# Letting the first up pass form its input factors three query blocks earlier, with two instead of three prepared weight blocks

## The chip, the cores and the metric

The kernel runs on one NeuronCore of a Trainium2 chip. The metric is device time in microseconds (us), the median over several runs of the whole program. Five engines work side by side, each on its own queue of instructions: TensorE (PE, matrix products; its weight loads are listed as PEld), VectorE (DVE), ScalarE (ACT), GpSimd (POOL) and SyncE (SP), which here issues all DMAs. PE writes its products to PSUM, in eight banks; all else lives in SBUF, where the kernel keeps 50 equal buffers that it calls units.

## What is computed

One layer of an encoder on 2048 positions of 1024 channels:

```
h = rms_norm(x) * (1 + sc_m) + sh_m
u, f, q, k, v = split(h @ w_in)
y = concat(s5_mixer(u), fourier_mixer(f), window_attention(q, k, v)) @ w_out
x = x + gt_m * rms_norm(y)
h = rms_norm(x) * (1 + sc_f) + sh_f
gate, val = split(dwconv3(h @ w_up))          # w_up: 1024 x 5632
x = x + gt_f * rms_norm((gelu(gate) * val) @ w_down)
```

The change concerns the place where attention ends and `h @ w_up` begins. Every product of float32 data is made of three float16 products (high by high, low by high, high by low), so each float32 tile is split once into a high and a low half: ACT makes the high half, DVE the low one.

## The kernel before

**Stages.** In the order of time: the input norm and the input projection, the S5 and Fourier mixers, attention, the output projection (`proj`), two up passes (`ffn`) and two down stages (`down`).

**Attention** (`att`) goes over 16 query blocks n of 128 positions; two workers take the even and the odd ones, with four PSUM banks between them. A block makes its scores on PE, adds the bias and takes the maximum on DVE (the `L1330` instructions), exponentials on ACT, splits on ACT and DVE, transposes on PE (evacuated by ACT and DVE in turn), the product with v on PE, and its evacuation by ACT (high) and DVE (low, the one `SCALAR_TENSOR_TENSOR` of shape 128x3x128). That evacuation sets the future `f_ya[n]`: "block n is out" below.

**Projection.** `proj` goes over four chunks c of 512 positions. Chunk c waits for `f_ya[4c]` to `f_ya[4c+3]`, then makes 192 products on PE. `post(c)` follows: it normalises, adds the residual, normalises again, mostly on DVE, and sets `f_hp[c]`.

**Up passes.** The products of `ffn` use seven instead of eight block products (a Strassen-Winograd form). Pass p takes chunks 2p and 2p+1. `hcomb(p)` forms the seven input factors of pass p: eight sums or differences and seven pairs of splits, in all 22 DVE instructions on 1024 columns each and 14 of ACT. `wcomb` forms the seven weight factors of one of 22 weight blocks i out of two 512 KB loads, with 8 DVE instructions, into four units (called W*i* below). Pass 0 forms them and also stores them; pass 1 loads them back (three loads of 512 KB and one of 256 KB). For each pass and block, PE makes 7 x 12 = 84 products of 128x512; `up_copy` (ACT) and three `up_add` (DVE) evacuate them; `up_act` does the convolution and the gate with five DVE instructions and stores the result. "Block i" below is an up block; query blocks are named as such.

**What sets the order.** A planner (`Sched`) runs all of these as generators against cost guesses, and emits instructions in the order of its clock, by priority; `yield ("w", f)` lets nothing behind it be emitted before f is set, `yield ("acq", sem, n)` takes n from a counting semaphore. The tile framework makes the queues of the engines from that. On the chip each engine then takes its queue in that order. The number of weight blocks in flight is the semaphore `lead`, with `W_LEAD` places, given back after the last product of a block. `hcomb(0)` starts when `post(0)` and `post(1)` are done and, as `H_GATE` is not 0, `f_ya[15]` is set.

The functions that the diff touches, with the line numbers of the profile:

Of the kernel before, what the change touches and what calls it, by code (L numbers as in the profile page):

```python
# [68 lines left out]
W_ON_V = 2  # L69
N_SL = 3  # L70
W_ADD, H_ADD, G_ADD, SSQ = "VVVV", "V", "VVVV", "V"
W_LEAD, W_RAW, U_PAIRS, D_LEAD, TAIL = 3, 1, 4, 6, 2
F_GATE, H_GATE, D_FROM = 0, 1, (1, 0, 2)
N_CH = 2
N_PE = (1,)
G_M2 = 8
# [126 lines left out]
class Builder:  # L203
# [1358 lines left out]
    def hcomb(self, p):  # L1562

        for i in range(2):
            yield ("w", self.f_hp[2 * p + i])
        (ya, ta), (yb, tb) = self.f_hp[2 * p].val, self.f_hp[2 * p + 1].val
        if p == 0 and H_GATE:
            yield ("w", self.f_ya[15])
        H = self.H[p] = {}
        if p:  # L1570
            self.f_ht = {r: [Fut(), Fut()] for r in (1, 5, 6, 2, 7, 3, 4)}
        t1_, t2_ = [self.u([2, 512]) for _ in range(2)], [self.u([2, 512]) for _ in range(2)]
        e = H_ADD

        def out(r, q, t, src):
            if q == 0:
                H[r] = [self.u([4, 512], F16) for _ in range(2)]
            sl = slice(2 * q, 2 * q + 2)
            t = yield from self.act(t, H[r][HI][:, sl], src, AF.Copy)
            t = yield from self.tt(t, H[r][LO][:, sl], src, H[r][HI][:, sl], ALU.subtract)  # L1580
            if q:
                self.f_H[p][r].set(t, H[r])
                if p:
                    for x in range(2):
                        t = yield from self.dma(t, self.h2d[r - 1, x].rearrange("p (a b) -> p a b", a=4), H[r][x])
                    self.f_h2[r].set(t)

        T = {}
        for q in range(2):
            T[1, q] = yield from self.tt(max(ta[q], tb[q]), t1_[q], yb[q], ya[q], ALU.subtract, eng=e)  # L1590
            yield from out(1, q, ta[q], ya[q])
        for q in range(2):
            tz = max(T[1, q], tb[q + 2])
            T[2, q] = yield from self.tt(tz, t2_[q], yb[q + 2], t1_[q], ALU.subtract, eng=e)
            yield from out(5, q, T[1, q], t1_[q])
        for q in range(2):
            T[3, q] = yield from self.tt(max(tb[q], tb[q + 2]), yb[q], yb[q + 2], yb[q], ALU.subtract, eng=e)
            yield from out(6, q, T[2, q], t2_[q])
        for q in range(2):
            yield from out(2, q, ta[q + 2], ya[q + 2])  # L1600
        for q in range(2):
            T[4, q] = yield from self.tt(max(ta[q + 2], T[2, q]), t2_[q], ya[q + 2], t2_[q], ALU.subtract, eng=e)
            yield from out(7, q, T[3, q], yb[q])
        for q in range(2):
            yield from out(3, q, tb[q + 2], yb[q + 2])
        for q in range(2):
            yield from out(4, q, T[4, q], t2_[q])
# [44 lines left out]
    def ffn(self):  # L1652
        A = self.A
        self.cwt, self.carry = self.const([P, 44, 4]), self.const([P, 44, 2])
        self.gx, self.wdd = self.const([P, 2, NFF]), self.dt([7, 11, P, 1024], F16)
        yield from self.dma(0, self.cwt, A["cw"])
        yield ("w", self.f_pc[F_GATE])
        wq, lead = [Fut() for _ in range(2 * NFF)], Sem(W_LEAD)
        self.sc.spawn(self.up_weights(wq, lead, Sem(W_RAW)))
        self.f_gr = [[Fut() for _ in range(NFF)] for _ in range(2)]  # L1660
        self.grd = self.dt([2, NFF, P, 1024], F32)
        self.f_up = [[Fut() for _ in range(NFF)] for _ in range(2)]
        self.f_wd = [Fut() for _ in range(11)]
        self.sc.spawn(self.down_weights(), 4)
        pairs = Sem(U_PAIRS)
        for p in range(2):
            fH = self.f_H[2 * p]
            gos = {}
            if p == 0:
                for r in (1, 5, 6, 2, 7, 3, 4):  # L1670
                    gos[r] = Fut()
                    self.sc.spawn(self.h_back(r, gos[r]), 0)
            for i in range(NFF):
                tp = yield ("acq", pairs, 1)
                tw = yield ("w", wq[NFF * p + i])
                W, ts = wq[NFF * p + i].val
                off = 1 + p
                U = [self.u([UB]) for _ in range(2)]
                n0, n1 = slice(off, off + 512), slice(off + 512, off + 1024)
                b1, b2, b3 = None, None, None  # L1680
                f = {r: Fut() for r in (1, 5, 6, 2, 7, 3, 4)}

                def prod(r, ps, t, first):
                    u, c = self.PLACE[r]
                    th = yield ("w", fH[r])
                    h = fH[r].val
                    t = max(t, th, ts[u])
                    for k in range(4):
                        sl = slice(k * P, k * P + P)
                        t = yield from self.mm3(t, ps, (W[u][:, HI, c, sl], W[u][:, LO, c, sl]),  # L1690
                                                (h[HI][:, k], h[LO][:, k]), first and k == 0, k == 3, r != 2)
                    if p == 0 and i == NFF - 1:
                        gos[r].set(t)
                    return t

                t = yield ("acq", self.bank["s"], 1)
                b1 = self.ps("s")
                t = yield from prod(1, b1, max(t, tp), True)
                self.sc.spawn(self.up_copy(t, b1, U[0][:, n0], f[1]))
                t = yield ("acq", self.bank["s"], 1)  # L1700
                b2 = self.ps("s")
                t = yield from prod(5, b2, t, True)
                self.sc.spawn(self.up_copy(t, b2, U[1][:, n1], f[5]))
                t = yield ("w", f[1])
                t = yield from prod(6, b1, t, False)
                self.sc.spawn(self.up_copy(t, b1, U[0][:, n1], f[6]))
                t = yield ("acq", self.bank["z"], 1)
                b3 = self.ps("z")
                t = yield from prod(2, b3, t, True)
                self.sc.spawn(self.up_add(t, b3, U[0][:, n0], f[1], f[2], True))  # L1710
                t = yield ("w", f[6])
                t = yield from prod(7, b1, t, False)
                self.sc.spawn(self.up_add(t, b1, U[1][:, n1], f[5], f[7], False))
                t = yield ("w", f[5])
                t = yield from prod(3, b2, t, False)
                self.sc.spawn(self.up_add(t, b2, U[0][:, n1], f[6], f[3], True))
                t = yield ("w", f[7])
                t = yield from prod(4, b1, t, False)
                self.sc.spawn(self.up_copy(t, b1, U[1][:, n0], f[4], True))
                lead.give(t)  # L1720
                self.f_up[p][i].set(t)
                self.sc.spawn(self.up_act(p, i, U, f, self.f_gr[p][i], pairs))
        yield from self.down()
# [386 lines left out]
```

## Time and profile before

| what | value |
|---|---|
| median of 3 runs | 2134.07 us (2133.83 to 2138.75) |
| the profiled execution | 2141.4 us, its span 2139.6 us |
| PE, DVE, ACT, POOL busy in the span | 1963.9, 1559.8, 991.0, 244.6 us |
| mean granted TensorE clock | 0.962 |
| query blocks 11, 12 and 15 out (DVE) | 767.3, 799.6, 840.3 us |
| both up passes end (PE) | 1701.8 us |

Times inside the span count from its first instruction. Busy time counts an engine while it executes. An idle stretch costs time only where it lies on the chain that ends last. In a row of the table by windows there stand, for one stretch, the busy time of each engine with the number of its instructions, the granted clock (1 is full speed) and the DMA share.

### The profile page before, as it was taken

What the parts mean: (1) busy time and instruction counts of PE and PEld (TensorE: products, weight loads), DVE (VectorE), ACT (ScalarE), POOL (GpSimd) and SP (SyncE); (2) the same over time, 40 slices, a digit from 0 to 9 for tenths busy, and PEclk for the clock granted to TensorE, in tenths of its full rate; (3) what the DMA queues carried; (4) which work ended last, traced back from release to release, by engine and by line L of the source; (5) the groups of instructions that cost most, each with busy time, mean ns of one, the idle gap of its engine ahead of it and who ended that gap; (6) DMA issues with size and microseconds to landing.
All of it is one profiled execution on the core that took longest, in us unless ns stands there. A gap on an engine that the chain in (4) does not pass through costs nothing.

```text
span 2139.6 us, 26850 instructions
## 1 busy us (share of the span) xinstructions
PE 1963.9 (92%) x9796; PEld 967.3 (45%) x9796; DVE 1559.8 (73%) x2305; ACT 991.0 (46%) x1666; POOL 244.6 (11%) x310
## 2 busy tenths in 40 slices
PE   6788888789988889997999999999999999999997
PEld 1336764444543444443444444444444444434445
DVE  8998898869677767899988875666565763547356
ACT  3643333355566576665555543444444433322221
POOL 1566554002000000000000000000000000011002
PEclk9989999899999989998999999999999999999998
DMA  9362145673746333346655566656565494548533
GB/s 368 105 209 61 56 127 162 217 247 137 256 144 220 126 125 133 136 179 249 223 197 187 188 216 260 230 189 226 201 217 201 158 334 157 162 134 300 177 100 113
DMA packets 206663, 397.27 MB, mean 186 GB/s; under 512 B 19521, under 2 KB 111938, under 8 KB 206530
## 3 DMA queue, kind: packets, MB, share of 16 engines
q1 hardware_dynamic: 206530, 395.55, 53.7%
q8 instruction: 77, 1.26, 0.2%
q14 instruction: 56, 0.46, 0.1%
HBM read 258.93 MB, written 134.98 MB: 184 GB/s over the span
## 4 chain that ended last, share of the span: by engine, by line
PE 49%; DVE 8%; ACT 2%; issue 1%; DMA 1%; POOL 0%; SPq 0%; POOLq 0%; DVEq 0%; ACTq 0%
PE ps L316 49%; DVE u L289 4%; DVE u L275 3%; ACT u L270 2%; DMA u<-d 0%; DMA u<-w_up 0%; DMA d<-u 0%; ACT L270 0%; POOL u L275 0%; SPq L265 0%; POOLq L2095 0%; DVE u L282 0%; ACT c L270 0%; DVEq L289 0%; DVEq L275 0%
## 5 line engine op out<-in xcount | busy, mean ns | idle before, releaser
L316 PE MATMUL ps<-u,u 128*128 128x512 f16 (+5 forms) x9030 | 1879.2, 368 | 90.7 <-DVE u L289 40.5
L316 PEld LDWEIGHTS <-u 128*128 128x128 f16 (+1 forms) x9058 | 846.8, 99 | 1035.4 <-issue 157.6
L275 DVE TENSOR_TENSOR u<-u,u 128x512 f32<-128x512 f32 (+10 forms) x584 | 506.6, 900 | 105.9 <-ACT u L270 92.4
L270 ACT ACTIVATE u<-u 128x1024 f16<-128x1024 f32 (+7 forms) x485 | 406.0, 869 | 360.9 <-DVE u L275 150.3
L270 ACT ACTIVATE u<-ps 128x512 f32<-128x512 f32 (+8 forms) x497 | 268.7, 555 | 410.4 <-PE ps L316 377.5
L289 DVE SCALAR_TENSOR_TENSOR u<-u,c,u 128x1023 f32<-128x1023 f32 (+5 forms) x248 | 291.3, 1197 | 61.2 <-ACT u L270 53.9
L289 DVE SCALAR_TENSOR_TENSOR u<-ps,u 128x512 f32<-128x512 f32 (+4 forms) x231 | 152.3, 666 | 229.2 <-PE ps L316 199.2
L289 DVE SCALAR_TENSOR_TENSOR u<-u,u 128x1024 f16<-128x1024 f32 (+6 forms) x225 | 240.6, 1093 | 61.4 <-ACT u L270 58.1
L275 POOL TENSOR_TENSOR u<-u,u 128x288 f32<-128x288 f32 (+9 forms) x169 | 187.4, 1123 | 609.3 <-DVE u L289 462.4
L270 ACT ACTIVATE u<-u,c 128x1023 f32<-128x1023 f32 (+3 forms) x106 | 123.5, 1166 | 142.5 <-DVE u L289 122.7
L305 POOL MEMSET u<- 128x1 f32 x88 | 8.6, 98 | 1118.0 <-DVE u L289 415.8
L270 ACT ACTIVATE u<-u,st 128x384 f32<-128x384 f32 (+3 forms) x192 | 107.5, 592 | 30.8 <-DVE st L282 17.3
L316 PEld LDWEIGHTS ps<-u,u 128*128 128x128 f32 (+1 forms) x532 | 91.1, 180 | 39.9 <-DVE u L275 16.8
L316 PE MATMUL ps<-u,c 128*128 128x512 f32 (+4 forms) x142 | 61.8, 551 | 43.5 <-DVE u L300 18.5
L316 PE MATMUL ps<-c,u 128*128 128x128 f16 (+1 forms) x568 | 59.6, 229 | 23.9 <-ACT u L270 18.5
L270 ACT ACTIVATE c<-u 128x2 f32<-128x2 f32 (+1 forms) x88 | 17.8, 202 | 132.3 <-DVE u L289 132.2
L275 DVE TENSOR_TENSOR u<-u 128x512 f32<-128x512 f32 (+8 forms) x136 | 67.8, 502 | 12.4 <-ACT u L270 11.6
L300 DVE TENSOR_TENSOR_SCAN u<-u,u 128x512 f32<-128x512 f32 (+1 forms) x60 | 68.6, 1152 | 0.5
L1330 DVE CUSTOM_DVE_ANT_0 u<-ps,u 128x384 f32<-128x384 f32 (+1 forms) x96 | 48.1, 536 | 23.8 <-PE ps L316 23.7
L289 DVE SCALAR_TENSOR_TENSOR u<-u,st,u 128x384 f16<-128x384 f32 (+1 forms) x96 | 54.6, 603 | 12.2 <-ACT u L270 12.0
L270 ACT ACTIVATE u<-u,c,c 128x512 f32<-128x512 f32 (+1 forms) x64 | 48.4, 804 | 22.3 <-DVE u L275 6.2
L316 PEld LDWEIGHTS ps<-u,c 128*128 128x128 f32 (+1 forms) x142 | 23.9, 190 | 72.6 <-issue 46.6
(52 smaller groups left out, 370.9 us busy)
## 6 DMA issues: line engine op xcount, KB each, us to landing
u<-d SPq DMA_DIRECT2D x226, 512.0 KB
d<-u SPq DMA_DIRECT2D x158, 512.0 KB
d<-u SPq DMA_DIRECT2D x111, 256.0 KB
u<-w_ada SPq DMA_DIRECT2D x48, 512.0 KB
u<-w_up SPq DMA_DIRECT2D x44, 512.0 KB
u<-d SPq DMA_DIRECT2D x66, 256.0 KB
u<-x SPq DMA_DIRECT2D x32, 512.0 KB
u<-d SPq DMA_DIRECT2D x24, 511.0 KB
```

The source lines that it names most:

```text
L270: self.S.activation(out, in_, func, **kw)
L275: (self.V if eng == "V" else self.G).tensor_tensor(out, a, b, op)
L289: self.V.scalar_tensor_tensor(out, a, s, b, op0, op1)
L300: self.V.tensor_tensor_scan(out, d0, d1, 0.0, ALU.mult, ALU.add)
L305: (self.V if eng == "V" else self.G).memset(out, v)
L316: self.PE.matmul(o, a, b, start=st, stop=sp, skip_group_check=chain)
L1330: V.tensor_tensor_reduce(out=s_, in0=o, in1=self.bias[h // 2][:, h % 2, bo:bo + nk * 128], op0=ALU.add, op1=ALU.max, scale=1.0, scalar=-3e ...
```

## The change

```diff
-W_LEAD, W_RAW, U_PAIRS, D_LEAD, TAIL = 3, 1, 4, 6, 2
-F_GATE, H_GATE, D_FROM = 0, 1, (1, 0, 2)
+W_LEAD, W_RAW, U_PAIRS, D_LEAD, TAIL = 2, 1, 4, 6, 2
+F_GATE, H_GATE, D_FROM = 0, 12, (1, 0, 2)
...
     def hcomb(self, p):
...
-        if p == 0 and H_GATE:
-            yield ("w", self.f_ya[15])
+        if p == 0:
+            yield ("w", self.f_ya[H_GATE])
...
     def ffn(self):
...
         pairs = Sem(U_PAIRS)
+        yield ("w", self.f_ya[15])
         for p in range(2):
```

`hcomb(0)` now waits for query block 12 instead of 15. The loop over up blocks gets a wait of its own for query block 15, which it had through the factors before. At most two weight blocks are in flight instead of three, in both passes. No instruction is added or removed; the planner puts them in another order.

On DVE's queue, from the evacuation of query block 12 on (the row of shape 128x3x128), stood the scores of query block 14 (L1330, 128x384) and evacuations of block 13's transposes:

```order
L289 SCALAR_TENSOR_TENSOR u_6411<-ps_6932,u_6410 128x3x128
L1330 ISA u_6982,st_6980<-ps_6981,u_3439 128x384
L1330 ISA st_6980 128x1
L1330 ISA u_6982,st_6980<-ps_6991,u_3439 128x384
L1330 ISA st_6980 128x1
L282 TENSOR_SCALAR u_6996<-ps_6997 128x512
L1330 ISA u_7008,st_6980<-ps_7007,u_3440 128x384
```

Behind the same evacuation stands now (u_4656, u_4657, u_5606 to u_5609 are the results of `post(0)` and `post(1)`):

```order
L289 SCALAR_TENSOR_TENSOR u_6388<-ps_6879,u_6387 128x3x128
L282 TENSOR_SCALAR u_6894<-ps_6914 128x512
L275 TENSOR_TENSOR u_6919<-u_5606,u_4656 128x1024
L275 TENSOR_TENSOR u_6639<-u_6639 128x512
L275 TENSOR_TENSOR u_6944<-u_4656,u_6943 128x1024
L275 TENSOR_TENSOR u_6920<-u_5607,u_4657 128x1024
L275 TENSOR_TENSOR u_6944<-u_4657,u_6943 128x1024
L275 TENSOR_TENSOR u_6921<-u_5608,u_6919 128x1024
L275 TENSOR_TENSOR u_6993<-u_6919,u_6992 128x1024
```

All 22 instructions of `hcomb(0)` stand there in one run, ahead of the scores of query block 14.

At the end of attention on the same queue, behind the last evacuation of query block 15, stood the first instructions of `hcomb(0)`:

```order
L282 TENSOR_SCALAR u_7364<-ps_7392 128x512
L289 SCALAR_TENSOR_TENSOR u_6411<-ps_7398,u_6410 128x3x128
L275 TENSOR_TENSOR u_7417<-u_5637,u_4656 128x1024
L275 TENSOR_TENSOR u_7437<-u_4656,u_7436 128x1024
L275 TENSOR_TENSOR u_7418<-u_5638,u_4657 128x1024
```

Now there stand the sums of squares of projection chunk 3 and `post(3)`:

```order
L282 TENSOR_SCALAR u_7453<-ps_7466 128x512
L289 SCALAR_TENSOR_TENSOR u_6388<-ps_7472,u_6387 128x3x128
L282 TENSOR_SCALAR u_7494<-u_7494 128x512
L275 TENSOR_TENSOR u_7494<-u_7494 128x512 x7
L289 SCALAR_TENSOR_TENSOR u_7765<-ps_7766,u_7765 128x512
L289 SCALAR_TENSOR_TENSOR u_7765<-u_7765 128x512
```

Between the last evacuations of query blocks 12 and 15 stand now, besides `hcomb(0)`, all 21 DVE instructions of `post(2)`, which stood behind query block 15 before. Weight block 2, which was formed ahead of query block 8, is formed after up block 0.

## The prediction

> **What bounds the kernel now.** I read the page's busy shares first, then the chain that ended last, then a table of windows cut at the marks around the change, and last the idle times on the timelines of PE and DVE.
>
> ```profile
> PE 1963.9 (92%) x9796; PEld 967.3 (45%) x9796; DVE 1559.8 (73%) x2305; ACT 991.0 (46%) x1666; POOL 244.6 (11%) x310
> 839.79 33.84 PE ps L316 x156
> 1067.76 634.07 PE ps L316 x2937
> ```
>
> PE is the bound over the whole span. The second and third line are pieces of the chain: from 839.79, when attention ends, the chain goes through PE, then for 200 us through DVE in small pieces, and from 1067.76 to 1701.83 through PE alone. A matmul there takes 634.07 / 2937 = 0.216 us and an up block of 84 takes 18.1 us. Whatever reaches 1067.76 later ends later by as much; nothing after it has slack. So the question is when the same work (9 up blocks done) is reached. The windows (us; then busy time of PE, PEld, DVE, ACT, POOL; granted clock; DMA):
>
> ```profile
> 739.55:767.27 27.72, 12.99 (x63) 7.04 (x63) 24.07 (x40) 17.94 (x35) 0.00 (x0) 0.57 0.33 113
> 767.27:799.53 32.26, 32.26 (x198) 16.99 (x197) 20.63 (x59) 28.39 (x63) 0.00 (x0) 1.00 0.43 131
> 799.53:815.93 16.40, 16.40 (x105) 8.92 (x104) 6.47 (x23) 6.23 (x18) 0.00 (x0) 1.00 0.22 73
> 815.93:833.22 17.29, 15.20 (x109) 8.58 (x106) 12.74 (x38) 14.65 (x38) 0.00 (x0) 1.00 0.67 235
> 833.22:840.25 7.03, 5.79 (x33) 2.95 (x34) 3.83 (x8) 3.69 (x8) 0.00 (x0) 0.76 0.49 168
> 840.25:900.77 60.52, 60.47 (x277) 27.33 (x276) 53.19 (x56) 37.73 (x51) 0.39 (x4) 1.00 0.35 122
> 900.77:927.30 26.53, 25.30 (x118) 11.33 (x116) 26.50 (x29) 15.17 (x22) 0.20 (x2) 1.00 0.39 149
> 927.30:949.10 21.80, 21.05 (x95) 9.20 (x94) 20.75 (x24) 16.78 (x24) 0.20 (x2) 1.00 0.55 193
> 949.10:979.22 30.12, 18.99 (x87) 8.29 (x86) 28.98 (x31) 17.35 (x24) 0.20 (x2) 0.86 0.51 204
> 979.22:1002.34 23.12, 21.28 (x87) 8.95 (x86) 21.12 (x24) 15.23 (x20) 0.39 (x4) 0.89 0.59 225
> ```
>
> The marks are DVE's: query blocks 10 to 15 out (first five rows), then the third `up_add` of up blocks 0 to 4. Two things are to be seen. From 799.5 to 840.3, the tail of attention, DVE works 23.0 of 40.7 us and waits the rest, while PE is nearly full, because projection chunk 2 fills it between attention's small products. From 840.3 to 900.8 PE is full (60.47 of 60.52), with projection chunk 3 and up block 0, and beside it DVE does `hcomb(0)` and `post(2)`. Then four up blocks take 101.6 us, of which DVE is busy 97.4, though PE needs only 4 x 18.1 = 72.4: there DVE is the bound.
>
> ```profile
> 752.22 0.29 PE L316 MATMUL ps<-c,u 128*128 128x128 f16 x1 [11.59 <-ACT u L270]
> 978.77 21.27 PE L316 MATMUL ps<-u,u 128*128 128x512 f16 x84 [10.70 <-DVE u L289]
> 1001.88 10.10 PE L316 MATMUL ps<-u,u 128*128 128x512 f16 x46 [1.84 <-DVE u L289]
> ```
>
> These are PE's longest waits there (idle time before the instruction, and what ended it, in brackets): two for DVE in the up blocks, and 11.59 us between query blocks 10 and 11, where `post(1)` sits in DVE's queue and no projection is left to fill PE. That place, the first window, is a model of what the change makes of the tail.
>
> **The change part by part.** First, what is moved into the tail. DVE takes its queue in order, so the run of `hcomb(0)` behind query block 12 is done before query block 14's scores. Because chunk 2 of the projection then ends before attention does, `post(2)` comes ahead of query block 15 too.
>
> ```profile
> 840.25 10.30 DVE L275 TENSOR_TENSOR u<-u,u 128x1024 f32<-128x1024 f32 x9
> 835.47 1.28 DVE L282 TENSOR_SCALAR u<-ps 128x512 f16<-128x512 f32 x2
> 869.49 0.43 DVE L282 TENSOR_SCALAR u<-u 128x512 f32<-128x512 f32 x1
> ```
>
> Nine 1024-column instructions take 10.30 us, 1.14 each; two of 512 columns take 1.28, 0.6 each in a row. Moved are 22 of `hcomb(0)` and 15 of `post(2)` at 1.14 = 42.2, and six smaller ones of `post(2)`, five at 0.6 and one at 0.4 = 3.4: 45.6 us. As a cross-check, the window 840.25 to 900.77 has 53.19 us in 56 instructions; 43 of these are the moved ones, and the other 13, of 512 columns at 0.6, are 7.8, which leaves 45.4.
>
> What of it lies beside waiting: the tail has 40.7 - 23.0 = 17.7 us of DVE gaps. If the moved work filled all of them, the tail would grow by 45.6 - 17.7 = 27.9; if none, by 45.6. The gaps come from the chain of each query block (PE, ACT and DVE in turn):
>
> ```profile
> 805.26 0.56 DVE L1330 CUSTOM_DVE_ANT_0 u<-ps,u 128x384 f32<-128x384 f32 x1 [5.65 <-PE ps L316]
> 814.96 0.17 DVE L275 TENSOR_TENSOR st<-st 128x6 f32<-128x6 f32 x1 [3.85 <-ACT u L270]
> 828.67 0.17 DVE L275 TENSOR_TENSOR st<-st 128x6 f32<-128x6 f32 x1 [3.04 <-ACT u L270]
> 839.78 0.56 DVE L289 SCALAR_TENSOR_TENSOR u<-ps,u 128x384 f16<-128x384 f32 x1 [3.02 <-ACT u L270]
> ```
>
> The first goes (PE will be long done), the last stays (nothing is left to put there), the two waits for exponentials stay in part, and ACT, with 14 splits of `hcomb(0)` and the affine steps of `post(2)` between, is slower to answer. In the model window DVE kept a gap of 27.72 - 24.07 = 3.7 us. I take about 6.5 for query blocks 13 to 15, less than three times the model's, as the run of `hcomb(0)` itself has no gap: 27.9 + 6.5 = +34.4, with ends of 27.9 and 45.6. Against it: in PE's new order 27 products of chunk 2 fewer stand ahead of query block 12's end (192 matmuls instead of 219 since query block 11's). At the 0.16 us per matmul of the window before 799.53 (32.26 / 198) that is -4.4. Query block 15 is out about 30 us later, near 870.
>
> Second, what is gained behind it. From query block 15 on PE needs chunk 3 and up block 0, 60 us whatever DVE does; DVE's queue has only 18 instructions there now (eight sums of squares of chunk 3, seven of `post(3)`, three `up_add`), some 12.5 us by the prices above, so its relief is hidden: 0. Between the third `up_add` of up blocks 0 and 4, DVE's queue holds 100 instructions instead of 102: weight blocks 2 to 5 instead of 3 to 6 (32 each), the same 32 of `up_act` and `up_add`, all 22 of `hcomb(1)` instead of 18, 14 of `post(3)` instead of 20. Four come at 1.14 and six go, four at 1.14, one at 0.6 and one at 0.4: -1, between -5 (better packing) and +5 (the two w_up loads stand behind stores of results on SP's queue, and a wait for one stops DVE). Behind up block 4 nothing of `hcomb(1)` is left on DVE; the last small waits of PE up to 1067.76 fall away, -2 (at most 2.4 by the timeline). PE's waits that cover the 200 us stay otherwise what they are.
>
> Third, weight block 2 no longer formed ahead of query block 8.
>
> ```profile
> 661.30:668.70 7.40, 6.55 (x31) 2.84 (x30) 6.78 (x8) 3.48 (x6) 0.00 (x0) 1.00 0.80 270
> ```
>
> That takes 6.8 us from DVE and 1 MB of loads from DMA, where PE is busy 6.55 of 7.40 us anyway: -0.5, between -6.8 and 0.
>
> Fourth, two blocks of weights in flight. In pass 0 a weight block is now finished within the up block just before its use, 5 to 10 us ahead. In pass 1 the reload takes the place of the previous block's:
>
> ```profile
> 1300.00:1400.00 100.00, 100.00 (x465) 45.38 (x464) 60.17 (x62) 42.64 (x67) 0.88 (x9) 1.00 0.60 209
> 1413.62 2.21 SPq L265 DMA_DIRECT2D u<-d  x4
> 1422.24 2.42 SPq L265 DMA_DIRECT2D u<-d  x4
> ```
>
> The four loads issued at 1413.62 feed pass 1's up block 8, which begins at 1701.83 - 14 x 18.1 = 1448, 34 us later; with one block less in flight they feed up block 7, 16 us later. 1.79 MB at even the mean 209 GB/s take 8.6 us, so the load hides; I take +0.5 for all 42 places, with 0 and +6 as ends.
>
> Last, the clock. PE is sparse in the longer tail, as in the model window, where the granted clock was 0.57. Behind the wait of 10.70 the window from 979.22 shows 0.89 over 23.12 us, 5 us at half rate, 2.5 lost. Chunk 3 begins right behind attention's own products, so I take +1.5. The Trainium skill ("TensorE: Matmul & The Clock Gate", Part 1: The HAM clock gate) says that an idle window of about 3.4 us drops the array to half rate; by it the gaps that this change opens would also slow attention's own matmuls, which is rival C below. The model window agrees on the rate, with 0.57.
>
> The sum: 34.4 - 4.4 - 1 - 2 - 0.5 + 0.5 + 1.5 = +28.5 us. On the profiled execution that makes 2141.4 + 28.5 = 2169.9; that one stands 7.3 above the median of 2134.07, so on the median it makes 2162.6. I say 2163.
>
> **The rivals.** A, faster: the first four up blocks are relieved. There PE waits some 18 us and runs some at half clock, worth about 20. If the tail filled all its gaps back to query block 11, it would be 43.7 (DVE busy in the four windows) + 45.6 - 4 (scores of query block 12 that now stand ahead of block 11's end) = 85.3 us against 73.0 elapsed, +12; together -8, 2126. For it speaks that PE waits for DVE there; against it that DVE's queue in these blocks shrinks by 1 us only. It decides if those 97 us fall under some 85: chance 0.05. B, a smaller loss: the tail packs as in A, the rest stays: +12, 2146. Against it stands that the waits for ACT belong to each query block: 0.12. C, the half clock lies on the chain: some 18 us of attention's PE work after query block 12 (37.4 in the three windows, less 88 products of chunk 2 at 0.216) doubles: +18, 2181. The model window, at 0.57, kept DVE's gap at 3.7 us, so most would hide: 0.08. D, two blocks starve an up pass: a load that lands more than 16 us after its issue stops PE; 1 us at each of 40 places is +40, 2203. PE at 100.00 with a lead of three says nothing on two: 0.07. The change does move what it says; the new order shows that.
>
> **How the numbers follow.** The likeliest, with 0.68, is the sum; its own ends are +16 (27.9 - 4.4 - 5 - 2.4) and +42 (45.6 - 4.4 and the clock), 2150 to 2176. The range takes in B below and half of C above: 2143 to 2180. A measurement tells about 0.3%, 6.4 us, from no change. Faster than that is A, 0.05; within it the weak end of B and some of A, 0.04; slower the rest, 0.91.
>
> **What would show it.** Right: query block 15 out near 870; PE idle some 30 us between 820 and 870; PE full for 60 us behind it; four up blocks that again take about 100 us; pass 1 without gaps. Wrong: query block 15 out before 855 (B), the four blocks in under 90 us (A), waits of PE for `DMA u<-d` or for DVE `wcomb` results behind up block 5 (D).

## The result, and the profile after

The changed kernel takes 2173.58 us (median of 4 runs, 2170.26 to 2174.66) against 2136.41 of the kernel before (4 runs, 2133.83 to 2140.11): ratio 1.017, 95% interval 1.0148 to 1.0192, 37 us slower. The forecast was 2163 in a range of 2143 to 2180; the sign and the size hold, but several of the terms behind them do not.

The first line is the page's busy shares (busy us, share, instructions); two long pieces of the chain follow (start, length, engine, line, count):

```profile
PE 1969.3 (91%) x9796; PEld 967.0 (45%) x9796; DVE 1560.9 (72%) x2305; ACT 997.2 (46%) x1670; POOL 241.9 (11%) x310
```

```profile
869.05 66.60 PE ps L316 x302
1065.16 666.59 PE ps L316 x3088
```

As before, the chain runs through PE from attention's end, then through small pieces of DVE, then through PE alone. Attention's end (839.79 before) comes 29 us later. ACT has four instructions more.

The windows, cut at the same marks (ends of the evacuation that puts a query block out, and of the third `up_add` of an up block): query blocks 10 to 15, up block 0, up block 4, up block 9, and a part of pass 1.

```profile
728.17:758.65 30.48, 18.03 (x91) 9.31 (x89) 27.35 (x54) 21.95 (x41) 0.00 (x0) 0.72 0.64 211
758.65:782.21 23.56, 23.22 (x147) 12.22 (x147) 16.21 (x43) 22.61 (x54) 0.00 (x0) 1.00 0.22 65
782.21:833.02 50.81, 34.86 (x174) 16.44 (x171) 41.23 (x59) 31.45 (x49) 0.00 (x0) 0.86 0.30 103
833.02:852.26 19.24, 12.35 (x64) 6.26 (x64) 16.57 (x30) 8.43 (x15) 0.00 (x0) 0.58 0.28 99
852.26:874.28 22.02, 9.43 (x47) 4.45 (x46) 12.15 (x25) 17.00 (x35) 0.20 (x2) 0.61 0.63 213
874.28:932.51 58.23, 58.23 (x270) 26.37 (x269) 13.42 (x19) 15.54 (x25) 0.20 (x2) 1.00 0.05 19
932.51:1030.42 97.91, 84.58 (x367) 36.52 (x366) 96.13 (x101) 63.71 (x86) 1.18 (x12) 0.96 0.60 226
1030.42:1120.44 90.02, 86.92 (x388) 38.58 (x387) 73.44 (x80) 48.28 (x70) 0.98 (x10) 0.96 0.53 195
1300.00:1400.00 100.00, 100.00 (x465) 45.40 (x464) 61.55 (x62) 43.59 (x68) 1.18 (x12) 1.00 0.71 261
```

Rows three to five are the tail, query block 12 to 15: 92.07 us instead of 40.72. PE works 56.64 of them and idles 35.4; before, it idled 3.3. DVE works 69.95 instead of 23.04, and its gaps have grown, from 17.7 to 22.1 us. The sixth row is the stretch behind attention, full on PE, with DVE busy for only 13.42 of 58.23 us, as forecast. The last shows pass 1 without a gap.

The same stretches of the kernel before, for the comparison below: query block 6 to 12, the tail, up block 0 to 4, up block 4 to 9.

```profile
642.36:799.61 157.25, 133.20 (x766) 68.34 (x766) 110.61 (x234) 107.56 (x217) 0.00 (x0) 0.90 0.48 158
799.61:840.33 40.72, 37.39 (x245) 20.47 (x244) 23.04 (x67) 24.66 (x61) 0.00 (x0) 0.96 0.46 157
900.86:1002.43 101.57, 86.62 (x380) 37.84 (x379) 97.34 (x103) 64.45 (x88) 0.98 (x10) 0.93 0.51 192
1002.43:1086.13 83.70, 81.29 (x376) 36.48 (x374) 77.00 (x84) 49.11 (x72) 0.98 (x10) 1.00 0.64 234
```

The account in us, from the marks of the two traces; from up block 9 on the distance stays at +34.3 to the end of pass 1. The forecast's +1.5 for the clock and +0.5 for pass 1 belong to no single row:

| stage | before | after | difference | forecast |
|---|---|---|---|---|
| up to query block 6 | 642.4 | 639.7 | -2.7 | 0 |
| query block 6 to 12 | 157.3 | 142.5 | -14.7 | -4.9 |
| query block 12 to 15 | 40.7 | 92.1 | +51.4 | +34.4 |
| query block 15 to up block 0 | 60.5 | 58.2 | -2.3 | 0 |
| up block 0 to 4 | 101.6 | 97.9 | -3.7 | -1 |
| up block 4 to 9 | 83.7 | 90.0 | +6.3 | -2 |

The first row is nothing of the change: over all traces here query block 6 is out between 639.1 and 644.3. So the comparisons below count from query block 6.

The longest waits of PE in the tail (idle time and what ended it in brackets):

```profile
814.89 1.44 PE L316 MATMUL ps<-u,u 128*128 128x384 f16 x4 [7.86 <-DVE st L1330]
827.53 3.64 PE L316 MATMUL ps<-u,u 128*64 128x384 f16 x14 [6.00 <-ACT u L270]
840.00 1.01 PE L316 MATMUL ps<-c,u 128*128 128x128 f16 x8 [3.69 <-DVE st L1330]
863.19 1.21 PE L316 MATMUL ps<-c,u 128*128 128x128 f16 x5 [10.79 <-ACT u L270]
```

The first is the run of `hcomb(0)`: the scores at 814.89 wait for banks that DVE empties only behind it. The last has `post(2)` ahead of it twice. Its pieces of the chain, in order:

```profile
852.26 1.28 ACT L270
853.56 0.60 ACT u L270
854.17 1.28 ACT L270
855.47 0.21 ACT st L270
855.68 6.91 ACT u L270 x18
862.63 4.62 ACT u L270 x9
867.30 1.08 PE ps L316 x7
```

The pieces of 1.28 us without a tile are loads of ACT's function table: each of `post(2)`'s two norms has one activation with a reciprocal root, it now stands between exponentials, and the table is changed to it and back. Behind query block 15's exponentials, from 859.05 on, eight affine steps of `post(2)` (5.9 us in three pieces) are mixed with the six splits for which PE waits. Among the groups by line of the tail (782.21 to 874.28) the loads have a row (count, busy us, mean ns, idle time before):

```profile
L270 ACT ACT_TABLE_LOAD x4 | 5.1, 1283 | 0.8 <-PE ps L316 0.7
```

They are the page's four added instructions of ACT, 5.1 us in all, each of them a piece of the chain: the program's text adds no instruction, but its new order does. The Trainium skill ("ScalarE activation tables: per-element evaluation and per-set limits", What a function is on this engine) says that two functions of different sets are one load of 1283 ns apart; the trace agrees, with a mean of 1283.

### The profile page after: what moved, and what is told of

Its sections match the earlier page's. It is cut to its first block, busy times and chain, and to the rows that moved or that the text cites. A ratio compares the mean times of both kernels' runs of the same rounds, so it can differ in the third digit from the quotient of the medians.

```text
span 2172.0 us, 26891 instructions
## 1 busy us (share of the span) xinstructions
PE 1969.3 (91%) x9796; PEld 967.0 (45%) x9796; DVE 1560.9 (72%) x2305; ACT 997.2 (46%) x1670; POOL 241.9 (11%) x310
## 4 chain that ended last, share of the span: by engine, by line
PE 54%; DVE 6%; ACT 2%; issue 1%; DMA 1%; POOL 0%; SPq 0%; POOLq 0%; DVEq 0%; ACTq 0%
PE ps L316 54%; DVE u L289 3%; DVE u L275 3%; ACT u L270 2%; DMA u<-d 0%; ACT L270 0%; DMA u<-w_up 0%; POOL u L275 0%; SPq L265 0%; DVE u L1330 0%; POOLq L2096 0%; ACT c L270 0%; ACT st L270 0%; DVE u L282 0%; DVEq L289 0%
## 5 line engine op out<-in xcount | busy, mean ns | idle before, releaser
L316 PE MATMUL ps<-u,u 128*128 128x512 f16 (+6 forms) x9030 | 1880.9, 369 | 100.2 <-DVE u L289 31.6
L316 PE MATMUL ps<-c,u 128*128 128x128 f16 (+1 forms) x568 | 61.8, 235 | 40.7 <-ACT u L270 31.8
L270 ACT ACTIVATE c<-u 128x2 f32<-128x2 f32 (+1 forms) x88 | 17.8, 203 | 135.7 <-DVE u L289 135.7
L1330 DVE CUSTOM_DVE_ANT_0 u<-ps,u 128x384 f32<-128x384 f32 (+1 forms) x96 | 48.0, 536 | 20.0 <-PE ps L316 18.0
```

What stands on the lines that cost most here:

```text
L270: self.S.activation(out, in_, func, **kw)
L316: self.PE.matmul(o, a, b, start=st, stop=sp, skip_group_check=chain)
L1330: V.tensor_tensor_reduce(out=s_, in0=o, in1=self.bias[h // 2][:, h % 2, bo:bo + nk * 128], op0=ALU.add, op1=ALU.max, scale=1.0, scalar=-3e ...
```

## The experiments

The theory after the result: the tail grows by the DVE work moved into it, with no gap to hide in; something else makes query block 12 early; and the lead of two costs a little in the up blocks. The change has three parts that can be separated: the lead, the wait of the loop over up blocks, and the place of `hcomb(0)`.

**The lead alone.** In the kernel before:

```diff
-W_LEAD, W_RAW, U_PAIRS, D_LEAD, TAIL = 3, 1, 4, 6, 2
+W_LEAD, W_RAW, U_PAIRS, D_LEAD, TAIL = 2, 1, 4, 6, 2
```

> The kernel before with two weight blocks in flight instead of three, and nothing else. Theory (the loss is the work moved into attention's tail; the lead costs nothing and its absence ahead of query block 8 gains): query block 8 is out some 9 us earlier than before (about 696 against 705.26), query block 15 about 831 against 840.33, the tail from query block 12 to 15 stays at 41 us, the up passes keep their pace, 2127 us (ratio 0.996). Rival one (two blocks in flight starve the up passes and are part of the loss): query block 15 as in the theory, but the up blocks fall behind, 2136 to 2155. Rival two (the gain ahead of query block 8 is idle time that the up blocks give back, since VectorE has weight blocks to form there): up block 4 ends as before at 1002, 2136.

Measured: 2139.98 us against 2136.56 (ratio 1.0015, 1.0003 to 1.0027). Windows: query block 6 to 12, up block 0 to 4, up block 4 to 9.

```profile
643.33:800.77 157.44, 133.48 (x766) 68.75 (x766) 104.92 (x226) 103.97 (x213) 0.00 (x0) 0.90 0.44 144
901.87:1003.07 101.20, 84.54 (x355) 36.07 (x354) 97.31 (x104) 64.46 (x88) 1.02 (x9) 0.92 0.51 193
1003.07:1090.71 87.64, 86.33 (x401) 38.98 (x399) 77.69 (x84) 49.39 (x72) 1.19 (x12) 1.00 0.62 224
```

The theory's gain is not there: without weight block 2 attention takes as long as before (157.44 against 157.25). And the lead costs: the first four up blocks, which DVE sets, take the same 101 us, but PE gets 355 matmuls done in them instead of 380: by the semaphore, the block after next is not formed yet. The 25 missing ones come behind, where PE is nearly full: 401 instead of 376, +3.9 us. That is once, not in every up block. The time lies in the range of rival one, but no load starves the up passes: from 1200 to 1300 us PE is busy 100.00 of 100.00.

**The loop's wait alone.** The kernel before with three blocks in flight and the new line in `ffn`, the factors behind query block 15:

```diff
+        yield ("w", self.f_ya[15])
         for p in range(2):
```

> The kernel before with the wait of the loop over up blocks for query block 15 alone: three weight blocks in flight, the input factors after query block 15. In the kernel before, the loop takes two units and one PSUM bank of attention's four ahead of query block 8 and then holds them until its factors are there; with the wait it takes them after attention. Theory (this gives the 8 us that query block 12 gained beyond weight block 2): query block 8 about as before (705), query block 12 about 8 us earlier (792 against 799.61), the tail at most as long as before, 2128 us (ratio 0.996). Rival (the wait changes nothing that lasts, and query block 12 came early only because products of chunk 2 were put behind it): query block 15 at 840, 2136.

Measured: 2138.69 us against 2136.56 (1.0005, 0.9995 to 1.0016). Query block 6 to 12, and the tail:

```profile
640.00:785.99 145.99, 118.02 (x662) 59.92 (x662) 102.25 (x216) 94.54 (x188) 0.00 (x0) 0.91 0.50 162
785.99:842.21 56.22, 55.14 (x344) 29.01 (x343) 31.10 (x85) 37.02 (x90) 0.00 (x0) 1.00 0.41 135
```

Query block 12 is 11 us earlier, but 344 matmuls instead of 245 are left for the tail, which PE fills for 56 us. Here the gain was borrowed from the tail, and the time is the rival's 2136 rather than the theory's 2128.

**Lead and wait together**, the changed kernel with the gate back at query block 15:

```diff
-F_GATE, H_GATE, D_FROM = 0, 12, (1, 0, 2)
+F_GATE, H_GATE, D_FROM = 0, 15, (1, 0, 2)
```

> The changed kernel with the input factors of the first up pass behind query block 15 again: lead of two and the loop's wait stay. Theory: up to query block 12 as in the changed kernel (out at 782), then the tail of the kernel before (41 us instead of 92.1), query block 15 out at 823, 60 us to up block 0 and four up blocks of 101.6 us, so 17 us less than before: 2119 us (ratio 0.992). Rival one (query block 12's early end is borrowed from the tail, which gets the products of chunk 2 that stood ahead of it): the tail takes 50 us, 2128. Rival two (the lead of two costs in the up passes): 2136 or more.

Measured: 2123.41 us against 2136.56 (0.9933, 0.9921 to 0.9946), faster than both kernels. Query block 6 to 12, the tail, up block 0 to 4, up block 4 to 9; then the one piece of its chain that covers the tail:

```profile
644.33:785.11 140.78, 124.56 (x733) 63.69 (x733) 101.70 (x224) 102.63 (x210) 0.00 (x0) 0.95 0.48 158
785.11:823.96 38.85, 38.85 (x273) 21.77 (x271) 23.58 (x67) 24.87 (x62) 0.00 (x0) 1.00 0.47 156
885.56:984.68 99.12, 86.57 (x367) 37.29 (x366) 96.53 (x102) 65.53 (x87) 1.22 (x10) 0.93 0.59 218
984.68:1072.36 87.68, 84.32 (x391) 37.97 (x389) 75.88 (x83) 48.41 (x70) 1.19 (x12) 1.00 0.57 212
```

```profile
773.31 61.95 PE ps L316 x405
```

So the changed kernel's early query block 12 is the work of these two parts together, and neither gains alone. And the tail with `hcomb(0)` behind it is PE's alone: 38.85 of 38.85 us, at clock 1.00, with DVE idle for 15.3 beside it. It is the base for the price of early factors: 92.07 - 38.85 = 53.2 us.

**What the wait sets free.** In `ffn` the loop takes two units, then one of attention's four banks, and then waits for its factors. Here the wait stands between the two:

```diff
                 U = [self.u([UB]) for _ in range(2)]
+                if p == 0 and i == 0:
+                    yield ("w", self.f_ya[15])
```

> As g15_lead_and_wait, with the loop's wait moved behind the place where the loop takes its two units, so that these are held through attention again and only the PSUM bank stays free. Theory (the bank is what attention gains by the wait; the queues of all engines stand as in g15_lead_and_wait): 140.8 us from query block 6 to 12 and 38.9 in the tail as there, 2123 us (ratio 0.9935). Rival (units are scarce, and two of them held cost attention the gain): 157 us from query block 6 to 12 as in the kernel before, 2137.

Measured: 2122.77 us against 2137.48 (0.9928, 0.9913 to 0.9944); 142.52 us from query block 6 to 12, 38.85 in the tail. With the units held the gain stays; without the wait (the lead alone) it is gone. In the code, what lies between the two places is the bank, so the bank is argued from the code; no trace here shows it held. Why three blocks in flight undo the gain was not settled: with a third block 4 more units are held, 8 instructions more of DVE stand in the queue, and the planner's order differs, all at once.

**`post(2)` out of the tail.** The changed kernel, with two lines in `post`, ahead of all its work:

```diff
+        if c == 2:
+            yield ("w", self.f_ya[15])
```

> The changed kernel with a wait for query block 15 at the start of post(2), so that of the moved VectorE work only hcomb(0) (22 instructions of 1.14 us, 25 us) stands in attention's tail and the 20.5 us of post(2) stand behind it, where the tensor engine has 60 us of products of its own. Theory (the tail grows by the VectorE work put there, gaps staying): the tail shrinks from 92.1 to about 72 us, query block 15 out at 854, 2153 us. Rival one (post(2) lay in waits for the exponentials and cost nothing; hcomb(0) alone is the 51 us): the tail stays near 90 us, 2172. Rival two (the half clock and the waits for ScalarE scale with the tail's length, so half of the moved work brings back less than half of the loss): tail 80 us, 2161.

Measured: 2143.48 us against 2136.56 (1.0029, 1.0018 to 1.0040). The tail, and up block 0 to 4:

```profile
784.60:850.46 65.86, 49.78 (x281) 26.49 (x279) 49.33 (x90) 40.57 (x78) 0.00 (x0) 0.84 0.29 100
909.26:1002.93 93.67, 80.72 (x341) 34.63 (x339) 90.46 (x96) 61.58 (x83) 0.89 (x9) 0.93 0.57 218
```

Taking 20.5 us of `post(2)` out shortens the tail by 26.2 us, more than the theory gave it, and the whole by 30. Of the 5.7 us beyond 20.5, 3.8 are table loads: the tail has one instead of four.

```profile
L270 ACT ACT_TABLE_LOAD x1 | 1.3, 1283 | 0.0
```

What is left, 25.1 us of `hcomb(0)`, still costs 65.86 - 38.85 = 27.0. The first four up blocks are relieved by 5.5 us against the kernel with lead and wait.

**The run cut in pieces**, `hcomb(0)` of the kernel above with waits for query blocks 13, 14 and 15 in it:

```diff
+        if p == 0:
+            yield ("w", self.f_ya[13])
         for q in range(2):
             T[3, q] = yield from self.tt(...)
```

> As p2_post_late, with hcomb(0) cut in four by waits for query blocks 12, 13, 14 and 15, so that VectorE's queue has 8, 7, 1 and 4 of its instructions behind these instead of 20 in one run. Theory (the run delays the next scores as a block, for which the tensor engine has no other work; in the tail of g15_lead_and_wait VectorE idles 15.3 of 38.9 us, which pieces can use in part): the tail is some 50 us instead of 65.9, query block 15 out at 835, 2130 us. Rival (each us of VectorE work in the tail costs a us wherever it stands, since every piece lies in the chain of a query block): 16 instructions of 1.14 in the tail, 57 us, 2137. Rival two (all pieces fill gaps): 42 us, 2122.

**Only the first piece early**, the next wait being for query block 15 already:

> As s3_spread, with only the first of the four pieces of hcomb(0) behind query block 12 (10 instructions with the two that hcomb(0) makes on chunk 1's tiles, 11.4 us) and the other twelve behind query block 15. Runs so far: 18.2 us of VectorE work in the tail cost 17.5, 25.1 cost 27.0 or 25.6, 45.6 cost 53.2. Theory (one for one from the first us: each piece stands in the chain of a query block): tail 50 us, query block 15 at 835, 2133 us. Rival (a threshold: VectorE idles 15.3 us of the 38.9, so a small dose is free): tail 40 to 42 us, 2123 to 2125 or, with the 4 us that s3_spread gained in the first four up blocks, 2120.

**A later gate**, the changed kernel with `H_GATE` 14, where `post(2)` falls behind attention by itself:

> The changed kernel with the input factors waiting for query block 14 instead of 12: 20 instructions of hcomb(0) in a run ahead of query block 15's last products, post(2) behind attention. Theory (the run's 22 us lie on query block 15's chain, and nothing else is left for the tensor engine but products of chunk 2): tail 62 us instead of 38.9 with the factors behind attention, query block 15 at 847, up block 0 58 us later, 8 us gained in the first four up blocks as in p2_post_late, 2138 us. Rival (the products of chunk 2 and what is left of attention cover half of the run): tail 50 us, 2127. Rival two (the place does not matter, only the volume and the waits for ScalarE count): as p2_post_late, tail 66 us, 2143.

Measured: 2138.45 us (1.0005, 0.9994 to 1.0016), 2124.84 (0.9948, 0.9932 to 0.9964) and 2143.56 (1.0024, 1.0014 to 1.0033). Their tails, in this order:

```profile
785.11:841.45 56.34, 47.81 (x276) 25.29 (x274) 44.51 (x86) 35.89 (x74) 0.00 (x0) 0.86 0.35 118
```

```profile
781.50:829.15 47.65, 45.14 (x281) 24.01 (x279) 35.18 (x77) 30.42 (x68) 0.00 (x0) 0.93 0.40 130
```

```profile
783.35:847.77 64.42, 46.15 (x281) 23.62 (x279) 48.97 (x90) 41.46 (x80) 0.10 (x1) 0.81 0.28 94
```

The moved instructions are counted in DVE's queue between query blocks 12 and 15, at 1.14 us each; the pieces hold 18 and the later gate 22, two more each than their expectations counted. The cost is the tail beyond 38.85 us. It is split into PE's idle time and what PE is busy longer than with lead and wait; it does 3 to 10 matmuls more there:

| kernel | moved DVE work, us | tail, us | cost | PE idle | PE busy longer | cost per us moved |
|---|---|---|---|---|---|---|
| first piece only | 11.4 | 47.65 | 8.8 | 2.5 | 6.3 | 0.77 |
| in pieces | 20.5 | 56.34 | 17.5 | 8.5 | 9.0 | 0.85 |
| gate at 14 | 25.1 | 64.42 | 25.6 | 18.3 | 7.3 | 1.02 |
| `post(2)` late | 25.1 | 65.86 | 27.0 | 16.1 | 10.9 | 1.08 |
| the change | 45.6 | 92.07 | 53.2 | 35.4 | 17.8 | 1.17 |

A threshold at the 15.3 us that DVE idled is out: 11.4 us already cost 8.8. Some 3 us may still be free, since the two smallest amounts cost 2.6 and 3.0 less than they are. At 25.1 us the place (gate 14 against 12) changes 1.4 us. What the cutting does is not separated from the smaller amount. Nor is DVE's work separated from ACT's: ACT's busy time in the tail rises with it, from 24.87 us to 30.42, 35.89, 41.46, 40.57 and 56.87 in the order of the table, and no run moves the one without the other. So the last column is the price of DVE's work with the ACT work that comes along.

In the smallest amount most of the cost is not idle time of PE, and DVE is hardly on the chain of its tail (PE has 80.7% of it, ACT 16.5%). Its last stretch, from query block 14 to 15, has a low clock:

```profile
820.06:829.15 9.09, 8.41 (x45) 4.34 (x46) 4.89 (x10) 4.75 (x11) 0.00 (x0) 0.62 0.69 230
```

For the pieces the first rival was right (57 us, 2137), for the later gate the second (66, 2143). The small dose lies between its theory and its rival in the tail, and its time, 2124.84, in the rival's 2123 to 2125. For 4.9 of the 8.8 us come back behind it: query block 15 to up block 0 and up block 0 to 4 take 58.93 + 96.94 us instead of 61.60 + 99.12 with lead and wait.

**The lead given back**, in three kernels that build on lead and wait: a third place is added when query block 15 is out, or 9, or 10.

```diff
         yield ("w", self.f_ya[15])
+        lead.give(self.f_ya[15].t)
         for p in range(2):
```

> As g15_lead_and_wait, and the third place of the lead is given back when query block 15 is out, so that attention has two weight blocks in flight and the up passes three. Theory (the lead of two costs some 4 us in up blocks 6 to 9, as e1_lead_two showed, and the third block is formed behind query block 15, where the tensor engine has 60 us of products of its own): query block 15 at 824, up block 0 at 886, the stage from up block 4 to 9 at 83.7 us instead of 87.7, 2119 us (ratio 0.992). Rival (weight block 2's 9 us on VectorE push post(2) and post(3) into the first up blocks, which wait for VectorE anyway, and take back what the later ones gain): up block 4 some 4 to 9 us later, 2123 to 2128.

> As g15_lead_and_wait, with the third place of the lead given back when query block 9 is out: weight block 2 (8 instructions of VectorE, about 8.5 us) stands ahead of query block 10. Theory (with three blocks formed the tensor engine runs ahead in the first four up blocks again, 376 matmuls instead of 401 from up block 4 to 9, worth 4 us; the 8.5 us lie in the stretch from query block 6 to 12, where VectorE idles 39 of 140.8 us, half hidden): 2123.4 - 4 + 4 = 2123. Rival one (one for one, as in the tail): 2128. Rival two (hidden altogether, as weight block 2 was ahead of query block 8, where its removal alone gained nothing): 2119.

> As t9_third_after_nine, given back when query block 10 is out: weight block 2 stands between query blocks 10 and 11, where the tensor engine's longest wait of attention lies (9.9 us for ScalarE in g15_lead_and_wait). Theory (that wait belongs to a chain of VectorE and ScalarE, and the work lengthens it one for one; 4 us come back in up blocks 4 to 9): 2123.4 + 8.5 - 4 = 2128. Rival (the wait is time that VectorE has to spare): 2119.

Measured: 2127.54 us (0.9949, 0.9936 to 0.9962), 2139.17 (1.0016, 1.0007 to 1.0025) and 2123.22 (0.9944, 0.9931 to 0.9957). First the kernel with 15, up block 0 to 4 and 4 to 9; then query block 6 to 12 of the one with 9; then of the one with 10, and its up block 4 to 9:

```profile
882.79:987.12 104.33, 86.39 (x376) 37.70 (x374) 102.36 (x109) 71.40 (x95) 0.98 (x10) 0.93 0.54 202
987.12:1070.84 83.72, 81.38 (x376) 36.48 (x374) 75.06 (x82) 47.48 (x70) 0.98 (x10) 1.00 0.61 223
```

```profile
642.90:795.17 152.27, 121.28 (x691) 61.44 (x691) 104.49 (x228) 101.74 (x207) 0.00 (x0) 0.89 0.48 158
```

```profile
640.02:786.67 146.65, 122.84 (x721) 62.97 (x721) 107.28 (x232) 104.77 (x212) 0.00 (x0) 0.92 0.51 167
987.49:1071.20 83.71, 81.29 (x376) 36.52 (x374) 77.00 (x84) 49.09 (x72) 0.98 (x10) 1.00 0.64 234
```

All three bring the stage from up block 4 to 9 back to 83.7 us, so the price of the lead stands. But weight block 2 has to be formed somewhere: behind query block 15 it lengthens the first four up blocks by 5.2 us, behind query block 10 attention by 5.9, behind query block 9 by 11.5 up to query block 12 and by 5.5 more in the tail. For 15 the rival was right (2123 to 2128); the time for 10 lies between its two expectations (2128 and 2119), and the time for 9 lies above all three of its own (at most 2128). Why 8.5 us of DVE work cost 17 us there was not settled. No place was found that beats 2123; the kernel with 10 only equals it.

## Why the prediction was right or wrong

**Right in sign and size, in part by luck.** The errors of the terms largely cancel: a loss was taken 17 us too small in the tail, and a gain ahead of it some 10 us too small. The moved work was counted right, 45.6 us in 43 instructions. The relief behind block 15 is hidden, as said: PE 58.23 of 58.23 us. The four up blocks take 97.9, near the 100 named. Pass 1 has no gap, so rival D is out: two blocks do not starve it. Rivals A and B are out, since the tail packs nothing.

**The step that failed most: "the tail has 40.7 - 23.0 = 17.7 us of DVE gaps", of which all but 6.5 fill.** The term was +34.4 with an upper end of 45.6; measured are +51.4 against the kernel before and 53.2 against the kernel with lead and wait. The idle time of DVE in the tail was no supply of time: 6.5 us of gaps were to be left, and 22.1 were. With lead and wait PE is the bound there, and DVE waits for it between steps of a chain on which PE's next products depend. The moved work, DVE's and ACT's, delays these steps. PE runs short of products of chunk 2: its idle time is 35.4 us, against 3.3 before and 0 with lead and wait. The small dose shows the loss at 11.4 us already, though there PE is busy longer more than it idles.

Beyond one for one, 7.6 us are left in the change (53.2 - 45.6). The table loads are 5.1 us of its chain, and the affine steps of ACT stand in it too; the prediction had named ACT as slower to answer but had no load in it. The rest may be the clock, which is rival C and for which the prediction's sum had +1.5. The granted clock of the three rows of the tail is 0.86, 0.58 and 0.61. PE's busy time there is 17.8 us more than with lead and wait, for 10 matmuls more (283, with the whole tail as one window). How much of it counts is bounded by the chain, in its shares for 800.10 to 869.05:

```profile
by line: ACT u L270 29.1%; DVE u L275 24.0%; PE ps L316 23.1%; ACT L270 7.4%; DVE u L289 7.3%; issue 7.1%; DVE u L1330 0.9%; DVE u L282 0.6%; ACT st L270 0.6%; DVE st L282 0.3%; DVE st L275 0.2%; DVE st L1330 0.2%; DVE st L1344 0.1%; ACTq L
```

PE holds 23.1% of 69.0 us, 15.9; were all of it at half rate, 8 would be lost. That estimate is an upper end for this chain, and no run here separates the clock from the rest.

**Query block 12: -4.4 and -0.5 forecast, -14.7 measured.** The steps named chunk 2's products and weight block 2. Up to query block 12 PE does 33 matmuls fewer (733 in the changed kernel as with lead and wait, 766 before), at the prediction's 0.16 us some 5 us, so the first step is near. Weight block 2 alone gains nothing, near the -0.5. The other 9 to 10 us come from the line that the prediction gave no term: the wait in `ffn`, which by the code leaves attention the bank that the loop had held, and which gains only together with the lead of two.

**The small waits up to up block 9: -2 and +0.5 forecast, +6.3 measured.** The lead was priced by what a reload has as slack in pass 1. Its cost lies in pass 0, in the stretch that DVE sets, where PE can run ahead only into blocks already formed: +3.9 us alone. In the changed kernel the windows show 388 matmuls instead of 376 and a clock of 0.96 instead of 1.00 there.

## What to carry to other kernels

An engine's idle time inside a chain of waits is not room for other work: before counting it as cover, ask whether the waiting engine stands between two steps of the engine that bounds the stage, and if it does, price moved work near one for one. Look in a change at each resource that a new wait releases (a bank, a buffer), not only at what it delays. When parts of a change have opposite signs, take them apart: here the lead and the loop's wait together make the kernel 0.7% faster, and the early factors lose 50 us on top of that (2173.58 against 2123.41).

## What the runs showed of the hardware

A load of ACT's function table costs 1283 ns each way, and one activation of another kind among exponentials brings two. In the sparse stretch of the changed kernel's tail the granted clock is half of the full one:

```profile
838.00:845.00 7.00, 3.31 (x22) 2.27 (x21) 7.00 (x11) 4.09 (x6) 0.00 (x0) 0.50 0.21 81
```

Four 128x128 products take 0.39 us with lead and wait, where the clock of the tail is 1.00, and 0.59 us in this stretch:

```profile
785.68 0.39 PE L316 MATMUL ps<-c,u 128*128 128x128 f16 x4
```

```profile
841.27 0.59 PE L316 MATMUL ps<-c,u 128*128 128x128 f16 x4 [0.26 <-ACT u L270]
```
